# Carrying the last cross-attention sample steps into the gated-linear-attention stage

## The chip, the cores and the metric

The kernel runs on one core of a Trainium2 chip. The time is device microseconds of one launch; runs of one kernel are compared by their median. Before the change three runs gave 1443.68 us in the median (1443.25 to 1445.27).

A core has a matrix engine (PE, with its weight loads shown apart as PEld), a vector engine (DVE), a scalar/activation engine (ACT), a general engine (POOL) and a queue that issues transfers (SP). Each works through its own list of instructions in order and waits on semaphores for the others. Matrix results land in PSUM; here PSUM is cut into six buffers called `px` and two called `pz`.

## The reference, cut to what matters

One layer of a hybrid decoder is computed for 1024 prompt tokens and for 8 sample tokens that share the weights but have caches of their own:

```python
h = rmsnorm(x, norm_gain)
proj = h @ w_in                       # one combined projection, split into 10 parts
br_gla  = gla(q, k, v, log_a, S0) * silu(gla_g)          # 4 heads, dk 128, dv 256
br_pool = multiscale_pool(u, hist) * silu(pool_g)
br_x    = cross_attn(xq, mem_k, mem_v) * silu(xg)        # 4 heads, 256 memory tokens
merged  = sum_n sigmoid(merge_n) * (branch_n @ w_branch_n)
y       = rmsnorm(x + merged @ w_out, final_gain)
```

For the prompt, keys and values of the cross branch come from `mem_prompt`; for each of the 8 samples they come from its own cache (`cache_mem_k`, `cache_mem_v`), so the cross branch of the samples is 32 small attentions (8 samples by 4 heads) with 256 keys each. The GLA of the samples is one step of the recurrence on `state_gla`. Everything is float32.

## The kernel before, in words

**The main stream.** The projection is done in 40 pairs of 128-column blocks. Each pair takes seven block products (a Strassen-like scheme, operands named `a11`, `a12`, `s2`, `s1`, `s3`, `s4`, `a22`), and each product is done in two halves of 12 matmuls into `px` tiles (L242 to L244: every product is three matmuls of high and low parts). DVE and ACT split the next operands ahead (L223, L224, L305), and SP loads the weights (`raw`, L296, three buffers).

**The side streams.** After each half, `fill()` is called, and it lets side streams issue some of their steps between the halves. The side streams are Python generators that yield a cost for each step. `streams[0]` runs `cross_steps()` and then `gla_steps()`: it is given 493 units of work (`WORK_A`) over the halves 28 to 357, so that about 1.5 units are issued after each half. The order of steps on PE and SP is thus written out by hand (these two engines keep the order of the program). On DVE, ACT and POOL a scheduler orders the instructions at compile time; on the chip they too run in that fixed order.

**The cross stage** runs over 16 pieces (4 heads by 4 blocks of 256 tokens) in rounds `s`, shifted against each other as a pipeline:

- `cross_scores(s)`: 12 matmuls into `pz`, softmax on DVE and ACT.
- `cross_weights(s-1)` (L724): four PE transposes of the softmax result into `pz`, split by ACT into `pTh` and by DVE into `pTl`.
- `cross_values(s-2)`: 12 matmuls from `pTh`, `pTl` and the values (`mvsh`, `mkv`) into `pz`, evicted by ACT as `xo` (L736).

Rounds 16 and 17 are the run-out of this pipeline: round 16 has `values(14)` and `weights(15)`, round 17 only `values(15)`.

**The samples' cross chain**, `cross_sample(h)`, is a second generator, of 87 steps for the four heads. Each round has five places (`yield next(samples, 0)`) where one of its steps is issued. For one head: loads of keys `kc` and of the query `qb` broadcast from `xqs`, products with them on DVE (L777), a transpose of the scores (L791) with a softmax on DVE and ACT (`nm`, `ps`, L793 to L798), a transpose of that (L803) into `pm`, loads of the values `vc`, twice 16 small matmuls (L817) with an eviction to `cs`, and a transpose (L827) copied into `brs`. Steps that hold nothing but a cost (`yield 0.5`) are there to leave time between an operation and what reads it.

**The GLA stage**, `gla_steps()`, has 17 rounds: `gla_load` (`alc`, `kq` by SP), `gla_gates` (one matmul pair L907, then a chain of DVE and ACT operations), `gla_within` (L944 to L946, `ak` split), `gla_recur`, `gla_out`. Its own sample chain, `gla_sample(h)`, of 65 steps, is issued at up to four places in a round; it begins with `gla_rows(0)` (L1001).

All of these use the two `pz` buffers in turn, a ring of 14 SBUF tiles (`R`), and four SBUF tiles (`V`) for the samples' loads.

Of the kernel before, what the change touches and what calls it, by code (L numbers as in the profile page):

```python
# [24 lines left out]
NH = 4  # L25
# [22 lines left out]
def trunk_kernel(ctx: ExitStack, tc: tile.TileContext,  # L48
# [628 lines left out]
    def perm8(ap):  # L677
        return ap.rearrange("p (i j) -> p i j", i=2)

    cross = {}  # L680

    def cross_load(h):
        cross["raw", h] = [loaded(mkv_scr[o][h], [2, DV], "mkv") for o in range(2)]
# [1 line left out]
    def cross_memory(h):  # L685
        mk, mv = cross["raw", h]
        t = PZ()
        for i in range(2):
            for a in range(2):
                nc.tensor.transpose(t[:, i * NM + a * P:i * NM + (a + 1) * P], mk[:, a, i * P:(i + 1) * P], ident)  # L690
        cross["mk", h] = split_r(t.rearrange("p (i m) -> p i m", i=2), [2, NM], "mkT")
        cross["mv", h] = split_in(mv, [2, DV], "mvs")
# [7 lines left out]
    def cross_scores(h, c):  # L700
        xh, xl = cross["q", h, c]
        mh, ml = cross["mk", h]
        t = PZ()
        for j in range(2):
            for i in range(2):
                cs = slice(j * P, (j + 1) * P)
                mm3(t[:, j * NM:(j + 1) * NM], xh[:, i, cs], xl[:, i, cs], mh[:, i], ml[:, i], i == 0, i == 1)
        nm = tiny(2, "nm")
        nc.vector.tensor_reduce(nm, t.rearrange("p (j m) -> p j m", j=2), axis=AX.X, op=ALU.max, negate=True)
        p = R([2, NM], name="p")  # L710
        sm = tiny(2, "sm")
        for j in range(2):
            act(p[:, j], t[:, j * NM:(j + 1) * NM], AF.Exp, bias=nm[:, j:j + 1], accum_out=sm[:, j:j + 1])
        nc.vector.reciprocal(sm, sm)
        for j in range(2):
            nc.vector.tensor_scalar(p[:, j], p[:, j], sm[:, j:j + 1], None, op0=ALU.mult)
        cross["p", h, c] = p

    def cross_weights(h, c):
        p = cross["p", h, c]  # L720
        t = PZ()
        for a in range(2):
            for j in range(2):
                nc.tensor.transpose(t[:, (2 * a + j) * P:(2 * a + j + 1) * P], p[:, j, a * P:(a + 1) * P], ident)  # L724
        cross["pT", h, c] = split_r(t.rearrange("p (a t) -> p a t", a=2), [2, CT], "pT")
# [106 lines left out]
    def cross_steps():  # L832
        def scores(n):
            cross_scores(n // 4, n % 4)

        def memory(n):
            if n % 4 == 0:
                cross_memory(n // 4)

        def weights(n):  # L840
            cross_weights(n // 4, n % 4)

        def values(n):
            cross_values(n // 4, n % 4)

        samples = chain_of(cross_sample(h) for h in range(NH))
        cross_load(0)
        cross_memory(0)
        cross_fetch(0, 0)
        yield 2  # L850
        cross_queries(0, 0)
        cross_fetch(0, 1)
        for s in range(16 + 2):
            if s < 16:
                scores(s)
                yield 3
                if s + 1 < 16:
                    cross_queries(*divmod(s + 1, 4))
                if s + 2 < 16:
                    cross_fetch(*divmod(s + 2, 4))  # L860
            if s % 4 == 2 and s < 14:
                cross_load(s // 4 + 1)
            if s >= 1:
                yield next(samples, 0)
            if 0 <= s - 2:
                values(s - 2)
                yield 1.7
            if s >= 1:
                yield next(samples, 0)
            if s % 4 == 3 and s < 15:  # L870
                memory(s + 1)
                yield 2
            if 0 <= s - 1 < 16:
                weights(s - 1)
                yield 1.7
            for _ in range(3):
                if s >= 1:
                    yield next(samples, 0)
        yield from samples

    def chain_of(gens):
        for g in gens:
            yield from g
# [122 lines left out]
    def gla_sample(h):  # L1006

        if h == 0:
            gla_rows(0)
            yield 1  # L1010
        t = PZ()
        nc.tensor.matmul(t[:, :NS], lhsT=w2[:, h * P:(h + 1) * P], rhs=als, start=True, stop=True)
        z, m = tiny(NS, "gz"), tiny(NS, "gm")
        gate_exps(t[:, :NS], NS, h, z, m)
        dec = wk.tile([P, NS], F32, tag="as", name="as", bufs=2)
        act(dec, m, AF.Exp, scale=1.0 / TAU)
        nc.vector.tensor_scalar(qm[:, :, 0], smp_of(S_Q + h)[:, 0], DK ** -0.5, None, op0=ALU.mult)
        yield 2
        ks = smp_of(S_K + h)[:, 0]

        def fetch(b0):
            s0 = loaded(st_gla[b0:b0 + 2, h].rearrange("b k v -> k b v"), [2, DV], "s0", V)
            vb = V([2, DV], name="vb")
            nc.sync.dma_start(out=vb, in_=v_scr[h][b0:b0 + 2].partition_broadcast(P))
            return s0, vb

        def states(b0, s0, vb):
            for i in range(2):
                b = b0 + i
                nc.scalar.activation(s0[:, i], s0[:, i], AF.Copy, scale=dec[:, b:b + 1])  # L1030
                nc.vector.scalar_tensor_tensor(s0[:, i], vb[:, i], ks[:, b:b + 1], s0[:, i], op0=ALU.mult, op1=ALU.add)
            nc.gpsimd.dma_start(out=o_gla_s[b0:b0 + 2, h].rearrange("b k v -> k b v"), in_=s0)
            return s0

        os_ = R([2, DV], name="os")
        sq = wk.tile([P, 2], F32, tag="sqs", name="sqs", bufs=2)
        for i in range(2):
            fetched = [fetch(4 * i + b0) for b0 in (0, 2)]
            yield 1
            yield 0.5  # L1040
            s0 = []
            for b0 in (0, 2):
                s0.append(states(4 * i + b0, *fetched[b0 // 2]))
                yield 1.5
            yield 0.5
            t = PZ()
            for j in range(4):
                nc.tensor.matmul(t[32 * j:32 * j + 32, :DV], lhsT=qm[:, 4 * i + j, :], rhs=s0[j // 2][:, j % 2, :],
                                 start=True, stop=True)
            nc.scalar.activation(os_[:, i], t[:, :DV], AF.Copy)  # L1050
            nc.scalar.activation(t[:, :DV], t[:, :DV], AF.Square, accum_out=sq[:, i:i + 1])
            yield 1
        if h + 1 < NH:
            gla_rows(h + 1)
        r = rstd_of(sq, 1.0 / DV)
        for i in range(2):
            nc.scalar.activation(os_[:, i], os_[:, i], AF.Copy, scale=r[:, i:i + 1])
        yield 1
        yield 0.5
        t = PZ()  # L1060
        for i in range(2):
            for d in range(2):
                nc.tensor.transpose(t[:, (2 * i + d) * P:(2 * i + d + 1) * P], os_[:, i, d * P:(d + 1) * P], ident)
        for d in range(2):
            nc.vector.tensor_scalar(perm8(brs[0][:, 2 * h + d]), column0(t, d), ggain[:, 2 * h + d:2 * h + d + 1], None,
                                    op0=ALU.mult)
        yield 1.2

    def gla_steps():
        samples = chain_of(gla_sample(h) for h in range(NH))  # L1070
        N = 16
        gla_load(0, 0)
        gla_load(0, 1)
        gla_gates(0, 0)
        gla_values(0, 0)
        yield 5
        for n in range(N + 1):
            h, c = divmod(n, 4)
            ph, pc = divmod(n - 1, 4)
            if n + 1 < N:  # L1080
                gla_gates(*divmod(n + 1, 4))
                yield 5
            if n < N:
                gla_split(h, c)
                gla_within(h, 2 * c)
                yield 2
            if n > 0:
                gla_recur(ph, 2 * pc + 1)
                yield 2
                yield next(samples, 0)  # L1090
            if n < N:
                gla_within(h, 2 * c + 1)
                yield 2
                yield next(samples, 0)
                if n + 2 < N:
                    gla_load(*divmod(n + 2, 4))
                if n + 1 < N:
                    gla_values(*divmod(n + 1, 4))
                gla_recur(h, 2 * c)
                yield 2  # L1100
            if n > 0:
                gla_out(ph, pc)
                yield 2
            for _ in range(2):
                if n >= 1:
                    yield next(samples, 0)
        yield from samples


# [368 lines left out]
    for hf, order in enumerate(ORDERS):  # L1478
        for tb in order:
# [23 lines left out]
            n, a = hf, 0  # L1503
            for b in ends:
# [14 lines left out]
                n, a = n + 1, b  # L1519
# [46 lines left out]
```

## Time and profile before

| | |
|---|---|
| median of three runs | 1443.68 us (1443.25 to 1445.27) |
| the profiled execution: its own time | 1445.01 us |
| the profiled execution: span from first to last instruction | 1443.3 us |
| granted PE clock over the span, mean | 0.997 |
| PE busy | 1417.4 us (98%) |
| DVE, ACT, POOL busy | 916.2, 679.0, 222.1 us |

PE is the bound nearly everywhere; the 26 us in which it is idle are at the beginning, at the end, and in the cross stage. A row of the timeline gives start, duration, engine, source line, operation, output and inputs, and in brackets the idle time before it and whom it waited for. The list of waits gives, for a line, the total time waited, how often and the longest. A row of windows gives the busy time of each engine in a stretch, the granted PE clock and the share of the DMA engines that were busy. Durations of matmuls overlap (they are pipelined), so the pace is read from starts, not from durations.

### The profile page before, as it was taken

The page shows a single profiled execution, that of the slowest core. Times are in us where ns is not written, and L with a number is a line of the kernel's source. Part 1 is how long each engine was busy: PE and PEld are TensorE (multiplying, and loading weights), DVE is VectorE, ACT ScalarE, POOL GpSimd, SP SyncE. Part 2 cuts the span into 40 slices and gives each one's busy share as a digit, 9 for nine tenths or more (in the row PEclk, how much of TensorE's full clock was granted, in tenths as well). Part 3 has the DMA queues.
Part 4 walks back from the last instruction along what each step waited for, and adds up shares of the span by engine and source line. Part 5 has one row for each costly group of instructions (what it writes and reads, how often), then busy time and mean ns, then how long its engine had stood idle before and what let it go on. Part 6 is the DMA issues. An engine that isn't in the chain of part 4 may idle for free.

```text
span 1443.3 us, 28179 instructions
## 1 busy us (share of the span) xinstructions
PE 1417.4 (98%) x10689; PEld 1356.1 (94%) x10689; DVE 916.2 (63%) x2123; ACT 679.0 (47%) x1575; POOL 222.1 (15%) x401
## 2 busy tenths in 40 slices
PE   8999999999999999999999999999999999999998
PEld 6899999989899999999999999999999999999876
DVE  6954756666687777767766778785672434554436
ACT  6743544443465666656654445444472432233212
POOL 3211111124342121212221111111010000000000
PEclk9999999999999999999999999999999999999999
DMA  9355665656656363554654455454694777632633
GB/s 329 125 165 169 217 218 187 207 175 165 198 155 193 115 192 129 182 176 126 187 167 150 149 188 170 159 184 163 204 298 134 234 257 249 234 104 79 224 118 116
DMA packets 183507, 259.42 MB, mean 180 GB/s; under 512 B 22204, under 2 KB 132564, under 8 KB 183364
## 3 DMA queue, kind: packets, MB, share of 16 engines
q1 hardware_dynamic: 159900, 183.87, 41.5%
q0 software_dynamic: 23328, 73.56, 14.7%
q8 instruction: 84, 1.38, 0.4%
q14 instruction: 51, 0.42, 0.1%
q10 hardware_dynamic: 144, 0.20, 0.0%
HBM read 180.47 MB, written 77.56 MB: 179 GB/s over the span
## 4 chain that ended last, share of the span: by engine, by line
PE 88%; DMA 5%; DVE 5%; issue 1%; ACT 1%; SPq 0%; POOL 0%; DVEq 0%; ACTq 0%; POOLq 0%
PE px L242 25%; PE px L243 25%; PE px L244 25%; DMA qb<-xqs 3%; PE pz L244 2%; PE pz L243 2%; PE pz L242 2%; DMA raw<-in_w_in_dram 1%; DVE kc L777 1%; PE pz L963 1%; PE pz L404 1%; PE pz L944 1%; PE pz L817 1%; PE pz L946 1%; PE pz L907 0%
## 5 line engine op out<-in xcount | busy, mean ns | idle before, releaser
L244 PE MATMUL px<-bh,wbl 128*128 128x384 f32 (+1 forms) x576 | 184.1, 320 | 0.0
L243 PE MATMUL px<-bl,wbh 128*128 128x384 f32 (+1 forms) x576 | 184.1, 320 | 0.0
L242 PE MATMUL px<-bh,wbh 128*128 128x384 f32 (+1 forms) x576 | 183.7, 319 | 0.0
L554 ACT ACTIVATE r<-px 128x258 f32<-128x258 f32 x240 | 89.9, 375 | 47.4 <-PE px L244 46.9
L242 PEld LDWEIGHTS px<-bh,wbh 128*128 128x128 f32 x576 | 108.3, 188 | 0.0
L243 PEld LDWEIGHTS px<-bl,wbh 128*128 128x128 f32 x576 | 108.2, 188 | 0.0
L244 PEld LDWEIGHTS px<-bh,wbl 128*128 128x128 f32 x576 | 108.2, 188 | 0.0
L242 PE MATMUL px<-ot,s1h 128*128 128x258 f32 x320 | 94.1, 294 | 0.0
L242 PE MATMUL px<-o,a12h 128*128 128x258 f32 x320 | 93.4, 292 | 0.0
L242 PE MATMUL px<-ot,s3h 128*128 128x258 f32 x320 | 93.2, 291 | 0.0
L242 PE MATMUL px<-o,s4h 128*128 128x258 f32 x320 | 93.0, 291 | 0.2 <-DVE c L636 0.2
L242 PE MATMUL px<-o,a11h 128*128 128x258 f32 x320 | 92.8, 290 | 0.0
L242 PE MATMUL px<-ot,a22h 128*128 128x258 f32 x320 | 92.6, 289 | 0.0
L242 PE MATMUL px<-ot,s2h 128*128 128x258 f32 x320 | 92.2, 288 | 0.0
L243 PE MATMUL px<-o,a11h 128*128 128x258 f32 x320 | 91.1, 285 | 0.3 <-DVE o L224 0.3
L243 PE MATMUL px<-o,a12h 128*128 128x258 f32 x320 | 91.1, 285 | 0.0
L244 PE MATMUL px<-o,a12l 128*128 128x258 f32 x320 | 91.0, 284 | 0.0
L244 PE MATMUL px<-ot,s1l 128*128 128x258 f32 x320 | 90.9, 284 | 0.0
L243 PE MATMUL px<-ot,s1h 128*128 128x258 f32 x320 | 90.8, 284 | 0.0
L244 PE MATMUL px<-o,a11l 128*128 128x258 f32 x320 | 90.6, 283 | 0.0
L243 PE MATMUL px<-ot,s2h 128*128 128x258 f32 x320 | 90.1, 281 | 0.5 <-DVE ot L224 0.5
L243 PE MATMUL px<-ot,a22h 128*128 128x258 f32 x320 | 90.5, 283 | 0.0
(471 smaller groups left out, 4634.3 us busy)
## 6 DMA issues: line engine op xcount, KB each, us to landing
raw<-in_w_in_dram SPq DMA_DIRECT2D x80, 512.0 KB, 4.0
msc<-c POOLq DMA_DIRECT2D x24, 516.0 KB, 4.8
brsc<-c POOLq DMA_DIRECT2D x24, 516.0 KB, 3.7
sig<-msc SPq DMA_DIRECT2D x24, 516.0 KB, 6.0
brr<-brsc SPq DMA_DIRECT2D x48, 256.0 KB, 5.2
wbr<-in_w_branch_dram SPq DMA_DIRECT2D x24, 512.0 KB, 5.5
acc<-sig POOLq DMA_DIRECT2D x16, 516.0 KB, 5.2
acc<-acc SPq DMA_DIRECT2D x16, 516.0 KB, 7.0
```

Of the source, the lines that this page charges most:

```text
L242: nc.tensor.matmul(out, lhsT=lh, rhs=rh, start=start, stop=False, skip_group_check=more)
L243: nc.tensor.matmul(out, lhsT=lh, rhs=rl, start=False, stop=False, skip_group_check=more)
L244: nc.tensor.matmul(out, lhsT=ll, rhs=rh, start=False, stop=stop, skip_group_check=more)
L404: nc.tensor.matmul(t[:, :DV], lhsT=memT[k // 2][:, k % 2, a * P:(a + 1) * P], rhs=raw[k // 2][:, k % 2], start=k == 0, stop=k == NK - 1)
L554: nc.scalar.activation(r, acc[c][:, :QT], AF.Copy)
L777: nc.vector.tensor_tensor_reduce(kc[:, a, :], kc[:, a, :], qb[:, bb, :], scale=1.0, scalar=0.0, op0=ALU.mult, op1=ALU.add, accum_out=sc[:, ...
L817: nc.tensor.matmul(t[32 * j:32 * j + 32, :DV], lhsT=pm[:, a, 4 * i + j, :], rhs=vc[j][:, a, :], start=a == 0, stop=a == 1)
L944: nc.tensor.matmul(t[0:64, 0:P], lhsT=ki[:, 0:64], rhs=qi, start=True, stop=True)
L946: nc.tensor.transpose(t[:, P:2 * P], kt, ident)
L963: nc.tensor.matmul(to, lhsT=kiqi[:, 1, cs], rhs=st, start=False, stop=True)
```

## The change

In the rounds 16 and 17 of the cross stage the three places at the end of the round are no longer taken, and what is left of the samples' chain after the last round is not run out there but handed over in the list `later`. The GLA stage issues it ahead of its own sample steps. There the places at the end of a round become three in the rounds 0 to 4 (in round 0 there were none), and stay two in the later ones.

```diff
-    cross = {}
+    cross, later = {}, []
...
-            for _ in range(3):
+            for _ in range(3 if s < 16 else 0):
                 if s >= 1:
                     yield next(samples, 0)
-        yield from samples
+        later.append(samples)
...
     def gla_steps():
-        samples = chain_of(gla_sample(h) for h in range(NH))
+        samples = chain_of(later + [gla_sample(h) for h in range(NH)])
...
-            for _ in range(2):
-                if n >= 1:
-                    yield next(samples, 0)
+            for _ in range(3 if n < 5 else 2):
+                yield next(samples, 0)
         yield from samples
```

## The prediction

> **What bounds the kernel now.** I read the page's totals first, then the list of PE's waits, then the timelines of PE, DVE, ACT and SP around the end of the cross stage, and last the windows for the clock.
>
> ```profile
> span 1443.3 us, 28179 instructions
> PE 1417.4 (98%) x10689; PEld 1356.1 (94%) x10689; DVE 916.2 (63%) x2123; ACT 679.0 (47%) x1575; POOL 222.1 (15%) x401
> PE   8999999999999999999999999999999999999998
> ```
>
> PE is idle for 1443.3 - 1417.4 = 25.9 us of the span. The change removes no operation and adds none, so it can only gain where PE waits or runs at a lower clock, and only between the end of the cross stage and the end of the GLA stage. PE's list of waits for that stretch:
>
> ```profile
> PE pz L803 <- DVE ps L798: 2.4, 1, 2.4
> PE pz L243 <- DVE pTl L224: 1.5, 1, 1.5
> PE pz L724 <- ACT xo L736: 1.1, 1, 1.1
> PE pz L1001 <- DVE ak L224: 0.7, 1, 0.7
> 400.00:420.00 20.00, 20.00 (x164) 19.22 (x163) 16.71 (x46) 13.39 (x38) 10.19 (x17) 1.00 0.58 142
> 450.00:500.00 50.00, 50.00 (x412) 47.60 (x412) 39.01 (x107) 31.49 (x87) 10.38 (x19) 1.00 0.42 131
> ```
>
> Four waits, 5.7 us together. After them PE is busy without a gap (20.00 of 20.00, 50.00 of 50.00), so the rest of the GLA stage has nothing to give. The four in PE's order of time, with the steps between them:
>
> ```profile
> 356.16 0.39 PE L243 MATMUL pz<-pTl,mvsh 128*128 128x256 f32 x1 [1.48 <-DVE pTl L224]
> 357.56 0.28 PE L242 MATMUL px<-o,a12h 128*128 128x258 f32 x1
> 358.99 0.38 PE L791 MATMUL pz<-ident,sc 128*8 128x128 f32 x2
> 360.47 0.66 PE L724 MATMUL pz<-ident,p 128*128 128x128 f32 x4 [1.11 <-ACT xo L736]
> 363.71 0.28 PE L244 MATMUL px<-ot,s2l 128*128 128x258 f32 x1
> 366.39 0.26 PE L803 MATMUL pz<-ident,ps 8*128 8x8 f32 x2 [2.39 <-DVE ps L798]
> 369.25 1.54 PE L817 MATMUL pz<-vc,pm 128*32 128x256 f32 x16
> 372.27 0.28 PE L242 MATMUL pz<-pTh,mvsh 128*128 128x256 f32 x1
> 376.67 1.07 PE L817 MATMUL pz<-vc,pm 128*32 128x256 f32 x16
> 379.22 0.60 PE L827 MATMUL pz<-ident,cs 128*128 128x128 f32 x4
> 381.10 0.59 PE L907 MATMUL pz<-alc,w 128*128 128x256 f32 x2
> 396.90 0.38 PE L1001 MATMUL pz<-ident,smp 128*8 128x128 f32 x2 [0.66 <-DVE ak L224]
> ```
>
> A half of 12 matmuls takes 358.99 - 357.56 = 1.43 us. What made the wait of 2.39 us so long is seen on DVE, ACT and SP:
>
> ```profile
> 355.06 0.42 DVE L777 CUSTOM_DVE_ANT_0 kc<-kc,qb 128x256 f32<-128x256 f32 x1 [4.10 <-DMA qb<-xqs]
> 358.58 0.69 DVE L305 TENSOR_TENSOR ws<-raw 128x512 f32<-128x512 f32 x1
> 359.30 0.37 SPq L296 DMA_DIRECT2D raw<-in_w_in_dram  x1
> 363.75 0.69 DVE L305 TENSOR_TENSOR ws<-raw 128x512 f32<-128x512 f32 x1 [2.75 <-issue]
> 364.69 0.40 DVE L793 TENSOR_REDUCE nm<-pz 8x1 f32<-8x256 f32 x1
> 365.59 0.57 ACT L223 ACTIVATE pTh<-pz 128x512 fp32r<-128x512 f32 x1
> 365.90 0.34 DVE L798 TENSOR_SCALAR ps<-ps,sm 8x256 f32<-8x256 f32 x1
> 366.19 0.69 DVE L224 TENSOR_TENSOR pTl<-pz,pTh 128x512 fp32r<-128x512 f32 x1
> 373.07 0.69 DVE L224 TENSOR_TENSOR a22l<-raw,a22h 128x512 fp32r<-128x512 f32 x1 [4.67 <-ACT a22h L223]
> ```
>
> DVE waits 4.10 us for the last query broadcast; that pushes back its L305 at 358.58, which frees the buffer into which SP issues the next weights at 359.30; these are not there until DVE has stood 2.75 us at 363.75. Behind that, in DVE's fixed order, stand the sample softmax (`nm`, `ps`) and the split `pTl` of the last prompt piece. So L803 is late because of a late weight load, not because it follows L791 too closely.
>
> **The change part by part.** *Where steps go.* Of the chain's 87 steps the five places of rounds 1 to 17 take 85 and the tail 2. With 6 places fewer, 8 steps pass over, costing 0.5+1.2+0.5+0.5+1.2+0.5+0.5+1.2 = 6.1 units: both L817, the second `vc` load, L827 and the empty steps. At 493 units over 357 - 28 = 329 halves (1.5 a half) the GLA stage starts 6.1 / 1.5, about 4 halves, earlier. Stepping through the yields, after the half that ends with L791 and L724 come: two halves, `values(15)`; one half, L803 with the first `vc` loads; one half, the GLA loads and L907. Before it was: two halves, L803; one half, L817; one half, `values(15)`. In GLA the carried steps come at halves 159 (L817), 166 (L817) and 172 (L827), `gla_rows(0)` moves from 161 to 173, and from round 5 on the chain of `gla_sample` runs one step behind the old one. Total work is the same, so the pool stage starts at the same half, 357.
>
> *The waits before (1.48 and 1.11 us): 0.* The steps up to L724 are issued in the old order, so both stay, and with them DVE's 4.10 and 2.75 us.
>
> *L803's wait: taken over by `values(15)`, +0.3 us.* `values(15)` stands where L803 stood, two halves behind L724. Its first matmul needs `pTh`, ready at 365.59 + 0.57 = 366.16; its second needs `pTl`, ready at 366.19 + 0.69 = 366.88, against `ps` at 366.24. At `values(14)` such a first matmul went ahead alone and the second waited (356.16). So the second starts at about 366.93 where L803 started at 366.39: 0.54 us later, less one matmul already done at the slow pace (about 0.2): +0.3. L803 then finds `ps` ready. Bounds: if DVE and ACT keep their order, +0.6 at most; if the split came ahead of the softmax in their order, the wait could vanish: -2.4. I take +0.3, since everything that these two engines are given ahead of that point is unchanged.
>
> *The clock behind that wait: 0.*
>
> ```profile
> 366.00:369.00 3.00, 2.61 (x14) 2.62 (x14) 2.36 (x5) 1.21 (x4) 0.00 (x0) 0.64 0.65 221
> 369.00:372.00 3.00, 3.00 (x28) 1.90 (x28) 0.00 (x0) 0.38 (x1) 0.00 (x0) 0.79 0.05 13
> 122.57 0.38 PE L242 MATMUL pz<-mkTh,xqsh 128*128 128x256 f32 x1 [1.39 <-ACT xqsh L226]
> 123.36 0.39 PE L244 MATMUL pz<-mkTh,xq 128*128 128x256 f32 x1 [0.29 <-DVE xq L227]
> 120.00:130.00 10.00, 7.78 (x48) 7.15 (x47) 5.81 (x13) 4.49 (x11) 0.95 (x2) 0.83 0.71 211
> ```
>
> The granted clock falls to 0.64 and 0.79 there: 3 x 0.36 + 3 x 0.21 = 1.7 us lost. It also fell after 1.39 + 0.29 us at 122.57 (0.83 over 10 us: the same 1.7 us), but not after the single 1.48 at 356.16. A wait of some 2.5 us at the same place is clearly on the falling side, so the 1.7 us stay. [...] I go by the row.
>
> *L1001's wait: -0.66 us.* `gla_rows(0)` asked for a `pz` buffer one half after the second `within`, before DVE had split the `ak` in it. Now an empty step takes that place and the next asker is `recur(0)`, two halves behind, which is 1.43 us later than L1001's ask and so past the 0.66. Bounds -0.66 and 0.
>
> *L817 and L827 in GLA: 0.* Their PE work is only moved (16, 16 and 4 matmuls). Their `vc` have 12 and 7 halves to land, at 3.8 us from issue to landing, and PE sees ACT's and DVE's small copies (`cs`, `brs`) only through the `pz` buffers. The one tight spot is half 172 to 173: L827, `gla_rows(0)` and `gates(3)` ask for three `pz` tiles within one half, so `gates(3)` waits if DVE's copy into `brs` is over 1.5 us late. Bounds 0 and the 0.66 that L1001 paid for such a turn; I take 0, since now DVE has one half to do it.
>
> *The GLA loads on SP's queue: 0.*
>
> ```profile
> 359.76 13.30 SPq L670 DMA_DIRECT2D vc<-in_cache_mem_v_dram  x8
> 374.21 0.50 SPq L898 DMA_DIRECT2D alc<-als  x1
> alc<-als SPq DMA_DIRECT2D x3, 128.0 KB, 4.6
> vc<-in_cache_mem_v_dram SPq DMA_DIRECT2D x8, 256.0 KB, 3.8
> ```
>
> Eight `vc` loads blocked SP until 373.06, the second four waiting for L817. Now only four stand ahead of `alc` and `kq`, so these go out at about 362 and land by 367. L907 comes after 366.93, eleven matmuls, two halves and L803, about 373: 6 us of cover. The next weight load no longer stands behind the second `vc` but behind seven GLA loads, over 10 us earlier. The second `vc` now blocks SP until L817 at half 159; the weights emitted behind it (before half 163) are for the pair that begins about 20 halves on. On DVE the first gates fall into the idle 4.67 us that end at 373.07. POOL's write of `v_scr` has 9 halves (13 us) until it is read, instead of 11.
>
> *Sum:* 0 + 0.3 + 0 - 0.66 + 0 + 0 = -0.3 us. The profiled execution took 1445.01 us (1.7 over its span of 1443.3), 1.3 above the median; on the median of 1443.68 this makes 1443.4 us.
>
> **The rivals.**
>
> *Faster: the gap closes.* If `values(15)` found its operands ready, because DVE and ACT get another order or the weights come sooner, the 2.39 us, the 1.7 us of clock and the 0.66 go: 1443.7 - 4.8 = 1438.9 us. For it: two halves and L803's old wait lie between L724 and the point of need. Against: DVE's 2.75 us at 363.75 stand ahead of both results. Chance 0.13.
>
> *The wait stays, the clock holds.* The gap is now cut in two (2.2 us, a matmul, then 0.4), which may leave the clock up: 1443.4 - 1.7 = 1441.7 us. Against it is 122.57, where a gap cut in two brought the clock down. [...] Chance 0.05.
>
> *Slower: `pz` at half 173.* The two `pz` buffers turn faster while carried steps, `gla_rows(0)` and gates mix with `recur` and `within`. If `gates(3)`, or a `recur` behind it, waits as long as L803 did, 2.39 us, the clock falls too: 1443.4 + 2.4 + 1.7 = 1447.5 us. It decides from a gap of about 1.7 us on, the 1.39 + 0.29 that brought the clock down. For it: DVE is at 16.71 of 20 us there. Against: between 400 and 500 us PE waited for nothing. Chance 0.12.
>
> *It does not matter:* `values(15)` costs a little more, and `recur(0)` takes over L1001's wait: 1443.7 to 1444.3 us. Chance 0.08.
>
> **How the numbers follow.** The forecast has the remaining 0.62; its own range goes from 1443.7 - 0.66 - 0.4 (how far the fastest run lies below the median) = 1442.6 to 1443.7 + 0.6 + 0.66 (the upper bounds at `values(15)` and at `gates(3)`, nothing gained at L1001) = 1445.0. About 0.2% (2.9 us) is what a measurement of this kernel can tell from no change. Faster by more is the first rival alone (0.13), slower by more the third (0.12), within it the rest (0.75). The range reaches down to the first rival (1438.8) and up to a slower case with its full gap short of the full clock loss (1446.4), which leaves out about 0.1.
>
> **What would show it right or wrong.** Right: PE's waits near 366 name `pTh` or `pTl` before L242 or L243 of `values(15)`, about 2.2 + 0.4 us; none at L803 or L1001; the window from 366 to 372 still has a clock below 0.85; L907 comes some 8 us earlier, near 373, without a wait. Wrong: no wait there and a clock of 1.00 (first rival), or a new wait at L907, L944, L963 or L1001 past 373, above all for `brs` or `ak` (third). If DVE's order ahead of 366 differs from the old one, the step that everything hangs on has failed.

## The result: 0.4% slower, and the profile after

The changed kernel took 1450.06 us in the median (1445.54 to 1454.55) against 1444.12 us for the kernel before, run beside it on the same chip (1442.29 to 1446.82): a ratio of 1.0037 (95% interval 1.0023 to 1.0050), or 5.9 us more. The forecast of 1443.4 us and its range, 1446.4 us at the widest, are missed on the slow side. The profiled execution took 1450.53 us, 5.5 us more than that of before. The first lines of its page:

```profile
span 1448.8 us, 28181 instructions
PE 1417.9 (98%) x10689; PEld 1356.5 (94%) x10689; DVE 916.1 (63%) x2123; ACT 680.2 (47%) x1575; POOL 221.0 (15%) x401
```

The work is the same, as it had to be: PE has 10689 matmuls and 0.5 us more busy time. The rest must be idle time or clock. PE's list of waits between 340 and 520 us (total, how often, longest):

```profile
PE pz L242 <- ACT pTh L223: 2.4, 1, 2.4
PE pz L243 <- DVE pTl L224: 2.0, 2, 1.7
PE pz L1063 <- DVE ak L224: 1.9, 1, 1.9
PE pz L907 <- DMA alc<-als: 1.2, 1, 1.2
PE pz L724 <- ACT xo L736: 1.1, 1, 1.1
PE pz L944 <- ACT pz L977: 0.4, 1, 0.4
```

Against the four waits of before: L803 and L1001 are gone, `values(15)` (L242, L243) has L803's, and three are new, at L907, L1063 and L944, with a small one of 0.2 us at L1012. (Of L243's 2.0 us, 1.70 are `values(14)`, which waited 1.48 before.) The timeline of PE shows the first part of it in order:

```profile
364.45 0.38 PE L242 MATMUL pz<-pTh,mvsh 128*128 128x256 f32 x1 [2.44 <-ACT pTh L223]
365.18 0.58 PE L243 MATMUL pz<-pTl,mvsh 128*128 128x256 f32 x1 [0.34 <-DVE pTl L224]
...
369.42 0.29 PE L803 MATMUL pz<-ident,ps 8*128 8x8 f32 x2
...
371.19 0.59 PE L907 MATMUL pz<-alc,w 128*128 128x256 f32 x2
...
393.82 0.67 PE L907 MATMUL pz<-alc,w 128*128 128x256 f32 x2 [1.15 <-DMA alc<-als]
```

and the windows the clock behind the first wait (us; busy PE, PEld, DVE, ACT, POOL; granted clock; share of the DMA engines; GB/s):

```profile
360.00:366.00 6.00, 3.21 (x22) 2.81 (x22) 3.83 (x9) 2.09 (x6) 2.16 (x4) 0.90 1.03 340
366.00:372.00 6.00, 6.00 (x41) 5.79 (x41) 0.83 (x3) 1.27 (x3) 0.68 (x1) 0.82 0.63 218
```

This is what was forecast: 2.44 + 0.34 us in place of 2.39, L803 without a wait, the clock down to 0.82, the first L907 ten microseconds earlier than before (371.19 against 381.10) and no wait at it. The third L907, at 393.82, is the first surprise. SP's queue, after and then before:

```profile
372.71 16.05 SPq L296 DMA_DIRECT2D raw<-in_w_in_dram  x2
388.85 0.66 SPq L898 DMA_DIRECT2D alc<-als  x1
```

```profile
387.60 0.45 SPq L898 DMA_DIRECT2D alc<-als  x1
...
400.70 0.59 PE L907 MATMUL pz<-alc,w 128*128 128x256 f32 x2
```

The gates of this piece came 6.9 us earlier (393.82 against 400.70), their load did not (388.85 against 387.60). It stands on SP behind two weight loads, and the second of these waits 15.6 us until DVE, with an L305 that ends at 388.36, has released its buffer. Of 13.1 us between issue and use, 5.0 are left, and 1.15 of them are a wait.

The larger piece is at 504 us. The rows of PE, then of DVE and ACT ahead of it:

```profile
487.57 0.64 PE L1048 MATMUL pz<-s,pm 128*32 128x256 f32 x8
...
491.36 0.60 PE L907 MATMUL pz<-alc,w 128*128 128x256 f32 x2
...
504.24 0.66 PE L1063 MATMUL pz<-ident,os 128*128 128x128 f32 x4 [1.88 <-DVE ak L224]
...
505.34 0.47 PE L944 MATMUL pz<-kiqi 128*64 128x128 f32 x1 [0.44 <-ACT pz L977]
```

```profile
493.82 0.69 DVE L305 TENSOR_TENSOR ws<-raw 128x512 f32<-128x512 f32 x1 [1.30 <-DMA raw<-in_w_in_dram]
...
494.43 0.15 DVE L265 SCALAR_TENSOR_TENSOR rr<-rq,rr 128x2 f32<-128x2 f32 x1
...
494.62 0.91 ACT L1057 ACTIVATE os<-os,rr 128x256 f32<-128x256 f32 x2 [2.47 <-DVE rr L265]
...
495.96 0.45 ACT L890 ACTIVATE bz<-pz,vec 128x256 f32<-128x256 f32 x1
...
496.69 0.48 DVE L891 TENSOR_SCALAR bz<-pz,vec 128x256 f32<-128x256 f32 x1
...
503.67 0.42 DVE L224 TENSOR_TENSOR ak<-pz,ak 128x256 fp32r<-128x256 f32 x1
```

The same pieces before:

```profile
491.58 0.60 PE L1063 MATMUL pz<-ident,os 128*128 128x128 f32 x4
...
492.01 0.60 PE L907 MATMUL pz<-alc,w 128*128 128x256 f32 x2
...
493.88 0.48 DVE L891 TENSOR_SCALAR bz<-pz,vec 128x256 f32<-128x256 f32 x1
...
500.74 0.42 DVE L224 TENSOR_TENSOR ak<-pz,ak 128x256 fp32r<-128x256 f32 x1
```

Read from the bottom up: L1063 asks for a `pz` buffer that DVE has not split into `ak`. `ak` is late because the gates are: from L907 to DVE's L891 it takes 5.3 us (491.36 to 496.69), before 1.9 (492.01 to 493.88). The gates are late because ACT stood 2.47 us at L1057, the scaling of `os`, ahead of L890. L1057 waited for `rr`, which stands on DVE behind an L305 that waited for weights. Before, the transposes behind that scaling (L1063) were already done at 491.58, ahead of the gates. So, as these rows read, a 0.15 us operation behind a late weight load holds up the gates of a whole round. Then the clock:

```profile
505.00:508.00 3.00, 2.66 (x14) 2.33 (x15) 2.40 (x11) 2.87 (x10) 0.00 (x0) 0.50 1.00 331
508.00:511.00 3.00, 3.00 (x16) 3.00 (x16) 0.55 (x2) 0.42 (x2) 0.94 (x2) 0.50 1.02 319
```

Half speed for 6 us: 3.0 us lost, and 0.4 us more at the edges (a clock of 0.85 from 504 to 505 and of 0.73 from 511 to 512). With the waits of 1.88 and 0.44 this is some 5.7 us. A last new wait is at the end of the samples' chain, where before L1063 found its data ready:

```profile
753.86 0.84 PE L1063 MATMUL pz<-ident,os 128*128 128x128 f32 x4 [1.04 <-ACT os L1057]
```

That these places are all of it can be tested by lining up the two traces: the same block products start in both. Just ahead of the border, at 344.56 against 346.77 us (`s4`), the trace of after is 2.2 us ahead. This is no gain of the change: it comes from the clock drop at 122 us, which this execution did not have (1.7 us, see the end), and from waits that differ between the two traces (0.97 us at 169, 0.96 at 293 and 0.98 at 308 before; 1.86 in all from 161 to 169, 0.39 at 292 and none near 308 after). Behind the last moved step, at 776.11 against 770.23 (`s1`), it is 5.9 us behind. So 8.1 us are lost in between, and the rows make 8.0 of them: 1.3 around the stage border (+0.2 at `values(14)`, +0.4 at `values(15)`, +1.15 at `alc`, -0.66 at L1001, +0.2 at L1012, nothing in the clock), 5.7 at 504 us, and 1.0 at the end of the chain. These are two single executions; the medians differ by 5.9 us.

### The profile page after: what moved, and what is told of

Read it like the earlier page. It is cut to its first block, busy times and chain, and to the rows that moved or that the text cites. A ratio compares the mean times of both kernels' runs of the same rounds, so it can differ in the third digit from the quotient of the medians.

```text
span 1448.8 us, 28181 instructions
## 1 busy us (share of the span) xinstructions
PE 1417.9 (98%) x10689; PEld 1356.5 (94%) x10689; DVE 916.1 (63%) x2123; ACT 680.2 (47%) x1575; POOL 221.0 (15%) x401
## 4 chain that ended last, share of the span: by engine, by line
PE 84%; DVE 6%; DMA 6%; ACT 2%; issue 2%; SPq 0%; DVEq 0%; POOL 0%; ACTq 0%
PE px L242 24%; PE px L243 24%; PE px L244 24%; DMA qb<-xqs 2%; PE pz L243 2%; PE pz L244 2%; PE pz L242 2%; DMA raw<-in_w_in_dram 2%; DVE kc L777 1%; PE pz L963 1%; PE pz L944 1%; DMA x<-in_x_prompt_dram 1%; DVE ws L305 1%; DMA vb<-vs 1%; PE pz L946 0%
## 5 line engine op out<-in xcount | busy, mean ns | idle before, releaser
L243 PE MATMUL px<-bl,wbh 128*128 128x384 f32 (+1 forms) x576 | 184.1, 320 | 0.0
L242 PE MATMUL px<-bh,wbh 128*128 128x384 f32 (+1 forms) x576 | 183.7, 319 | 0.0
L242 PEld LDWEIGHTS px<-bh,wbh 128*128 128x128 f32 x576 | 108.3, 188 | 0.0
L243 PEld LDWEIGHTS px<-bl,wbh 128*128 128x128 f32 x576 | 108.2, 188 | 0.0
L242 PE MATMUL px<-o,a11h 128*128 128x258 f32 x320 | 94.9, 297 | 0.0
L242 PE MATMUL px<-ot,s1h 128*128 128x258 f32 x320 | 93.5, 292 | 0.0
L242 PE MATMUL px<-o,s4h 128*128 128x258 f32 x320 | 92.7, 290 | 0.2 <-DVE c L636 0.2
L242 PE MATMUL px<-ot,s3h 128*128 128x258 f32 x320 | 92.7, 290 | 0.0
L242 PE MATMUL px<-o,a12h 128*128 128x258 f32 x320 | 92.6, 289 | 0.0
L242 PE MATMUL px<-ot,s2h 128*128 128x258 f32 x320 | 92.4, 289 | 0.0
L243 PE MATMUL px<-o,a11h 128*128 128x258 f32 x320 | 92.1, 288 | 0.3 <-DVE o L224 0.3
L242 PE MATMUL px<-ot,a22h 128*128 128x258 f32 x320 | 92.1, 288 | 0.0
L243 PE MATMUL px<-ot,s2h 128*128 128x258 f32 x320 | 90.1, 282 | 0.5 <-DVE ot L224 0.5
L243 PE MATMUL px<-ot,a22h 128*128 128x258 f32 x320 | 90.5, 283 | 0.0
L243 PE MATMUL px<-ot,s1h 128*128 128x258 f32 x320 | 90.5, 283 | 0.0
L243 PE MATMUL px<-o,a12h 128*128 128x258 f32 x320 | 90.5, 283 | 0.0
L244 PE MATMUL px<-ot,s3l 128*128 128x258 f32 x320 | 90.4, 283 | 0.0
```

What stands on the lines that cost most here:

```text
L242: nc.tensor.matmul(out, lhsT=lh, rhs=rh, start=start, stop=False, skip_group_check=more)
L243: nc.tensor.matmul(out, lhsT=lh, rhs=rl, start=False, stop=False, skip_group_check=more)
L244: nc.tensor.matmul(out, lhsT=ll, rhs=rh, start=False, stop=stop, skip_group_check=more)
```

## Experiments

The theory that they began with (A): from round 5 on the samples' chain stands one step behind its old place, this puts the scaling of `os` just ahead of the gates and the L1063 behind it in front of a late `ak`; undo the lag and the loss goes. Its rival, the prediction's third: the two `pz` buffers simply turn faster with another asker among them, whatever ACT and DVE do there. A second question was the price of giving `values(15)` L803's wait, and a third whether the delay behind that wait can be removed in another way. All ratios are against the kernel before in runs beside it (its median was 1443.44, 1443.81, 1442.43 and 1443.53 us in the four groups e1 to e4, e5 to e8, e9 to e11, e12 to e14).

### e1: the lag undone by a place in round 0

```diff
-            for _ in range(3 if n < 5 else 2):
+            for _ in range(4 if n == 0 else 3 if n < 5 else 2):
```

> The changed kernel with four instead of three places at the end of GLA round 0, so that from the end of round 4 on every step of the GLA samples stands where it stood before the change. Theory A (the changed kernel loses its time because the samples' chain runs one step behind: the step that scales `os` now stands right ahead of the gates of round 6, ACT waits there for DVE, the gates and the split of `ak` come late, and PE waits at L1063 and L944 for 1.9 + 0.4 us, plus 3.4 us of clock): the waits near 504 us are gone, the clock there is 1.00, and the time is 5 to 6 us below the changed kernel, about 1444 to 1445 us. Theory B (it is the earlier start of the GLA stage, with the gates that wait for `alc`, and what follows from it): still 1448 to 1451 us.

1448.25 us, ratio 1.0038 (1.0024 to 1.0052). The waits at 504 are gone (PE is busy without a gap from 485 to 520 us, at a clock of 1.00), but another wait has come:

```profile
395.61 3.63 PE L817 MATMUL pz<-vc,pm 128*32 128x256 f32 x16 [4.66 <-DMA vc<-in_cache_mem_v_dram]
```

The fourth place of round 0 puts the second L817 right behind the first, before its `vc` can land. The time therefore says nothing about the lag; the trace says that the wait at 504 depends on which steps stand there.

### e2: half of the change, fewer places, nothing carried

```diff
-            for _ in range(3):
+            for _ in range(3 if s < 16 else 0):
```

> The kernel before with only the six places of the cross rounds 16 and 17 taken away; the samples' chain is run out ahead of the GLA stage, which is as before. Theory A: no loss from the GLA samples, since their steps stand as before; values(15) waits for pTh and pTl in place of L803 (about 2.4 + 0.3 us), and L1001 waits about 0.7 us as before: 1443.5 to 1446 us, the 8 steps run one after the other adding at most 1 us. Theory B: also no loss, as GLA starts at its old half. A time above 1447 us would mean that the cross part alone costs something that neither theory has.

1446.92 us, ratio 1.0023 (1.0009 to 1.0037), above the expected 1443.5 to 1446. The rest of the chain now runs out right behind `values(15)`, and its loads have no time to land:

```profile
PE pz L817 <- DMA vc<-in_cache_mem_v_dram: 2.2, 3, 1.3
```

So the carry does what it says for `vc`: in the changed kernel no L817 waits.

### e3: the lag alone

```diff
-        samples = chain_of(gla_sample(h) for h in range(NH))
+        samples = chain_of([[0]] + [gla_sample(h) for h in range(NH)])
```

> The kernel before with one empty step of no cost at the head of the GLA samples' chain, so that its steps come one place later throughout and nothing else changes. Theory A: a wait of 2 to 2.5 us appears at L1063 and L944 in GLA round 5 (near 500 us) with the clock at one half for some 6 us: 1448 to 1450 us. Theory B: no change, 1443 to 1445 us.

1444.05 us, ratio 1.0003 (0.9992 to 1.0014): theory A falls. The old kernel with one empty step ahead of its chain has no wait at 504 us. What differs is the neighbourhood: here L1048 (the matmuls of the samples' outputs, whose result is scaled) runs four halves ahead of the scaling, in the changed kernel one half. The third place in round 4, the last round that has three, packs L1048, the scaling and the gates of round 6 one behind the other. This is theory A' below: not the lag, the crowding. The lag does cost something, at the end of the chain:

```profile
747.37 0.84 PE L1063 MATMUL pz<-ident,os 128*128 128x128 f32 x4 [0.74 <-ACT os L1057]
```

### e4 and e5: the scaling left out, and the place moved away

The changed kernel without the scaling of `os` for head 0, whose output is then unscaled:

```diff
-        r = rstd_of(sq, 1.0 / DV)
-        for i in range(2):
-            nc.scalar.activation(os_[:, i], os_[:, i], AF.Copy, scale=r[:, i:i + 1])
+        if h > 0:
+            r = rstd_of(sq, 1.0 / DV)
+            for i in range(2):
+                nc.scalar.activation(os_[:, i], os_[:, i], AF.Copy, scale=r[:, i:i + 1])
```

> The changed kernel without the normalisation of `os` for head 0 of the samples (the small chain for its reciprocal root and the two scalings on ACT, about 1 us of ACT work, are left out for that head); all steps stay at their places and L1063 still asks for its `pz` between recur and within. Theory A: ACT no longer waits for DVE ahead of the gates of round 6, `ak` is split in time, the waits near 504 us are gone: 1444 to 1445.5 us. Rival C (the turn of the two `pz` buffers: the mere request of L1063 between recur and within makes PE wait, however the gates run): the wait at L1063 stays, 1449 to 1451 us.

1446.09 us, ratio 1.0017 (1.0008 to 1.0026). Its list of waits from 340 to 520 us has no L1063 any more:

```profile
PE pz L907 <- DMA alc<-als: 2.5, 1, 2.5
PE pz L242 <- ACT pTh L223: 2.2, 1, 2.2
...
PE pz L944 <- ACT pz L977: 1.0, 1, 1.0
```

L1063 still asks for `pz` at the same place between the same askers, so the rival (the turn of the buffers by itself) is out as the cause of that wait: it came through the scaling. (L944 still waits for a buffer, 0.97 us here.) The trace also parts the scaling from the late weights ahead of it. L305 stood 2.40 us for its weights here, longer than the 1.30 us of the changed kernel, and yet L890 began 0.7 us after L907 (491.84 to 492.58) instead of 4.6 us (491.36 to 495.96). So late weights alone do not hold up the gates; whether the scaling would with weights in time was not run. The same with all work in place, the changed kernel with its last third place moved from round 4 to round 2:

```diff
-            for _ in range(3 if n < 5 else 2):
+            for _ in range(4 if n == 2 else 3 if n < 4 else 2):
```

> The changed kernel with its five extra places at other rounds: four at the end of round 2 and two at the end of round 4, instead of three and three. From round 4 on every step of the GLA samples then stands where it stood in the kernel with only the lag of one step, so L1048 of head 0 comes four halves ahead of the step that scales `os` instead of one, while that step and L1063 keep their places (halves 213 and 220). Theory A' (not the lag, but L1048, the scaling and the gates of round 6 following one another closely, because of the third place in round 4): the waits at L1063 and L944 near 504 us and the clock drop go, 4 to 6 us below the changed kernel: 1444.5 to 1446.5 us, with the wait for `alc` and the one at values(15) left. Theory A (the lag): unchanged, 1449 to 1451 us.

1446.50 us, ratio 1.0020 (1.0004 to 1.0037). From 485 to 520 us PE is busy without a gap at a clock of 1.00. What is left at the border, beside `values(15)`:

```profile
PE pz L907 <- DMA alc<-als: 2.6, 1, 2.6
```

### e6 and e8: the loads of the gates brought forward

The changed kernel with the loads of GLA piece 2 issued right behind the gates of round 1, and then the same together with the moved place:

```diff
                 gla_gates(*divmod(n + 1, 4))
+                if n == 0:
+                    gla_load(0, 2)
...
-                if n + 2 < N:
+                if 0 < n < N - 2:
```

> The changed kernel with the three loads of GLA piece 2 issued right behind the gates of round 1, seven halves earlier, so that on SP they stand ahead of the weight load that waits for DVE. Theory B: the wait of L907 for `alc` (1.2 us in the changed kernel, 2.5 us in the kernel without the scaling of head 0) goes, and with it the clock drop that follows it in part of the runs: 1 to 3 us below the changed kernel, 1447 to 1449 us. If that wait does not matter: unchanged, about 1450 us.

> The changed kernel with both edits, the place moved from round 4 to round 2 and the loads of GLA piece 2 ahead of the weight load. If these two make up the loss: the time of the kernel before or a little less, 1442.5 to 1444.5 us, with the wait at values(15) as the only long one left after 350 us. If something else of the carry costs time: above 1446 us.

Alone: 1449.93 us, ratio 1.0043 (1.0028 to 1.0058), no gain. The wait for `alc` is gone, L1063's 1.89 us at 504 stays, and a new one comes right behind. Its cause was not followed further; in e8, whose steps up to there are the same, it is 0.33 us.

```profile
402.41 1.07 PE L817 MATMUL pz<-vc,pm 128*32 128x256 f32 x16 [1.55 <-ACT pz L977]
```

With the place moved: 1445.02 us, ratio 1.0015 (1.0002 to 1.0029), the best form of the carry. After 350 us PE's list has only the following, 1.1 at L724 and 0.69 at the last L1063:

```profile
PE pz L242 <- ACT pTh L223: 2.3, 1, 2.3
PE pz L243 <- DVE pTl L224: 1.4, 2, 1.1
...
PE pz L817 <- ACT pz L977: 0.3, 1, 0.3
PE pz L1012 <- DVE ak L224: 0.2, 1, 0.2
```

This kernel and e6 differ by the place alone and ran beside each other; the ratio of their means is 0.9973 (0.9953 to 0.9994, worked out from the spread of both), so the place in round 4 is worth 3.9 us (1 to 7), which has room for the 5.7 of the trace. What the `alc` wait is worth stays open: from the moved place alone to both it is 0.9993 (0.9973 to 1.0012).

### e7, e9, e10 and e11: time given to the late split instead

The kernel before with an empty step between `weights(15)` and what follows, to see whether the wait at L803 can be bought off without any carry. First 3 units more in all; then 1.5 and 3, taken back from the first cost of the GLA stage (`yield 5`), so that GLA starts at its old half:

```diff
                 yield 1.7
+                if s == 16:
+                    yield 3.0
```

> The kernel before with 3 units of empty cost (two halves of products, 2.9 us) put in between weights(15) and L803; what follows comes two halves later. If the reading of that wait is right (the softmax and pTl are late by a fixed time, because of a late weight load), L803 finds its operand there: its 2.4 us and the 1.7 us of clock behind it go, 4 us below the kernel before: 1439 to 1441 us. If the wait only moves with the step (the results come later too): 1443 to 1445 us.

> The kernel before with 1.5 units of empty cost (one half, 1.43 us) between weights(15) and L803, and 1.5 units less behind the first gates of the GLA stage, so that from the gates of round 1 on all steps stand where they stood. If the wait at L803 is a fixed lateness of DVE (and the loss with two halves of gap came from the shift of everything behind): its 2.4 us become about 1.0 us, under what brings the clock down, so 1.4 + 1.7 us are gained: 1440.5 to 1442 us. If the results move with the step: 1443.5 to 1444.5 us.

> The same with 3 units (two halves) at both places: the wait at L803 goes altogether, as it did with the gap of two halves before, and the steps from the gates of round 1 on stand as before, so the waits that came with that shift (the hist load, ak and others) are not there: 1439.5 to 1441 us. Against it stands that the first gates now have 5 instead of 7 halves until within(0); if they are late by then, PE waits 0.5 to 3 us there and the time is 1441 to 1444 us.

The first took 1454.28 us, ratio 1.0085 (1.0072 to 1.0098): no wait at L803 any more, but everything in GLA stands two halves later, and from 520 us on PE waits twice for `ak` (3.6 us) and for the pool stage's load:

```profile
PE pz L1129 <- DMA hist<-in_state_pool_dram: 4.6, 1, 4.6
```

With the units taken back: 1442.75 us, ratio 0.9997 (0.9983 to 1.0012), and 1442.13, ratio 1.0003 (0.9991 to 1.0015), no difference that shows: the first lies between its two expectations, the second in the range of its worse one. With 1.5 units the wait has been shared out (lines behind 875 have moved by two, so L1003 is the old L1001):

```profile
PE pz L1003 <- DVE ak L224: 1.4, 1, 1.4
...
PE pz L817 <- DMA vc<-in_cache_mem_v_dram: 1.0, 1, 1.0
...
PE pz L803 <- DVE ps L798: 0.6, 1, 0.6
```

With 3 units the trace has no wait at L803 and no clock below 1.00 from 354 to 400 us. Its waits there are 1.6 us at L1003 and 1.1 each at L243 and L724, 3.8 us in place of the 5.7 and the 1.7 us of clock in the kernel before. The times do not show these 3.6 us: the interval leaves room for a gain of 1.3. The profiled execution was the shortest of its twelve (1437.88 us), and one and the same wait brings the clock down in some traces only (see the end); whether this explains it stays open.

Then the best form of the carry with the 1.5 units ahead of `values(15)`, taken back in the same way:

> The changed kernel with the place moved to round 2, the loads of GLA piece 2 ahead, and the gap of 1.5 units, here between weights(15) and values(15), with 1.5 units less behind the first gates. If the wait at values(15) is the same fixed lateness as that at L803: from 2.3 + 0.3 us to about 1.2 us and mostly without the clock drop, 2.5 to 3 us below the kernel without the gap: 1442 to 1443 us. If not: 1444.5 to 1445.5 us.

1448.68 us, ratio 1.0041 (1.0030 to 1.0053). `values(15)` waits only 0.45 + 0.34 us, and the first gates, at the place where the prediction had 6 us of cover, wait for their load, which went out only at 365.32, behind a weight load at 364.91:

```profile
369.03 1.19 PE L909 MATMUL pz<-alc,w 128*128 128x256 f32 x2 [3.62 <-DMA alc<-als]
```

### e12 to e14: the root of the waits, the last query broadcast

If the late `qb` load (DVE's 4.10 us in the prediction's rows) is what makes the split late, a kernel without it has no wait to take over, and the carry is measured by itself. For the last pair of samples of head 3 the query tile of the pair ahead is used, one load of 256 KB less:

```diff
-        def fetch(b2):
+        def fetch(b2, old=None):
...
+            if old is not None:
+                return kc, old
...
-                kcs, qb = fetch(b2 + 1)
+                kcs, qb = fetch(b2 + 1, qb if h == 3 and b2 == 2 else None)
```

> The kernel before, but the last pair of samples of head 3 uses the query tile of the pair ahead of it, so that one load of 256 KB (`qb`) is left out. Theory D (all four waits of PE between 354 and 367 us come down from DVE's wait of 4.1 us for that load, which makes the split, the eviction, the next weight load and the softmax late): DVE's wait at L777 shrinks to 1 us or less, the waits at values(14), L724 and L803 (1.5, 1.1 and 2.4 us) mostly go with the clock drop behind them: 1437.5 to 1440 us. If each of them has a cause of its own: at least two stay, 1441.5 to 1443.5 us.

> The changed kernel with the same load left out. The wait at values(15) (2.4 + 0.3 us, with the clock) should go like that at L803. Theory A' (the loss lies in round 4's third place, at L1063 near 504 us) and B (`alc` behind the weight load): their waits stay, as they do not hang on that load, and the distance to the same edit on the kernel before stays at 4.5 to 6 us: 1443 to 1445.5 us. If the loss comes down from the late data at values(15): the distance shrinks to 2 us or less, 1439 to 1441.5 us.

> The changed kernel with the place moved to round 2, the loads of GLA piece 2 ahead, and the same load left out. Without these two causes and without the late data there is nothing known left that the carry costs: within 1 us of the same edit on the kernel before, 1437.5 to 1440.5 us. If it stays 1.5 us or more above, the carry has a cost that no wait seen so far explains.

On the kernel before: 1440.26 us, ratio 0.9976 (0.9964 to 0.9988), 3.3 us less, which counts only as a measure of the waits since a load, and its traffic, is missing. For the kernel before the root is shown: `values(14)` and L724 no longer wait, and L803 waits 0.5 us, for another operation (L805 is the old L803, L1003 the old L1001). What stays is

```profile
PE pz L1003 <- DVE ak L224: 0.7, 1, 0.7
PE pz L805 <- ACT r L554: 0.5, 1, 0.5
```

The traces differ by 6.2 us there (5.7 of waits and 1.7 of clock against 1.2), the medians by 3.3 (by the interval 1.7 to 5.2).

On the kernel after: 1445.46 us, ratio 1.0017 (1.0005 to 1.0030). The new waits of the GLA stage are still there:

```profile
PE pz L909 <- DMA alc<-als: 2.1, 1, 2.1
PE pz L1065 <- DVE ak L224: 1.9, 1, 1.9
```

`values(15)` waits only 0.79 + 0.45 us in this trace, and the clock stays at 1.00 from 360 to 372 us. So without the late query the carry costs 5.2 us (1445.46 - 1440.26; with it 5.9): the main loss is the carry's own and does not come from the wait that it was laid around.

The carry with moved place and early loads: 1441.60 us, ratio 0.9992 (0.9981 to 1.0002), 1.3 us above the same edit on the kernel before (with the query 1.2), a little more than the 1 us expected. But here the late data are not gone: DVE waits 2.28 us for a load of keys (`kc`) instead, `values(15)` waits 1.46 + 0.34 us, and the clock is 0.50 from 363 to 366. So this run does not settle what the best form would cost with data in time.

## Why the prediction was wrong

*The waits before* and *L803's wait: taken over by `values(15)`*: right. The first two waits stayed (1.70 and 1.09 against 1.48 and 1.11), the third was taken over at +0.4 us (forecast +0.3), and DVE kept its order up to the split.

*The clock behind that wait*: right for this execution. 6 x 0.10 + 6 x 0.18 = 1.7 us lost between 360 and 372, as before. But the second rival (the clock holds) is not out: in the trace of e4 the clock stayed at 1.00 behind 2.22 + 0.34 us at the same place.

*L1001's wait: -0.66*: right, it is gone. A wait of 0.2 us for `ak` is new at L1012.

*The GLA loads on SP's queue: 0*: wrong. The step checked the first two pieces, whose loads had only four `vc` ahead of them, and was right for them (no wait at 371.19). It had the next weight load go out over 10 us earlier, but that load went out at 372.71, 1.1 us earlier than before (373.79): it waits for DVE to release a buffer, and DVE had moved forward by no more than that (its `a22l` at 371.99 against 373.07). From the third piece on the GLA loads stand behind such weight loads, while L907 had moved 6.9 us forward: 1.15 us here, 2.1 to 2.6 in e4, e5 and e13. The price in the median stays open.

*"From round 5 on the chain of `gla_sample` runs one step behind the old one"*: this sentence carried no price, and was the place of the loss. The working followed the moved steps L817 and L827 through *`L817 and L827 in GLA: 0`*, and these cost nothing indeed. It did not ask what the steps of `gla_sample` meet at their new places: the term that was left at 0 is +5.7 us at 504 in the trace (3.9 by the runs of e8 against e6), from the scaling of `os` between L1048 and the gates, and +1.0 at the end of the chain. The lag of one step alone is not the fault, as e3 shows; it takes the third place in round 4 beside it, as e5 shows. That PE waited for nothing between 400 and 500 us was read as room to spare; it did not say how near DVE and ACT were to being late there.

The third rival had the kind of loss right (a wait for a `pz` buffer, then the clock, 1447.5 us), with a chance of 0.12, but put it at half 173, where L827, `gla_rows(0)` and `gates(3)` meet and nothing waited. The gap of about 1.7 us from which it let the clock fall is not a limit: the same gap at 122 us left the clock at 0.83 in the trace of before and at 1.00 in that of after.

The sum of the best form: +0.24 at `values(15)` (2.29 + 0.34 - 2.39), -0.66 at L1001, +0.33 at L817, +0.2 at L1012 and +0.7 at the last L1063 is +0.8 us, against 1.2 by the medians (by the ratio's interval 0.3 to 4.2). So even without the two mistakes the change gave nothing that could be measured: it passes a wait from one instruction to the next, and the delay is made on DVE and in the loads.

## What to carry to other kernels

When steps of a hand-ordered chain are moved, every later step of the chain moves too: look, for each of them, at what DVE and ACT have queued around its new place, above all for a small operation (here 0.15 us) that stands behind a load and ahead of something that many wait for. An engine that moves forward takes its need for loads forward, not the loads (here the third gates came 6.9 us earlier and the issue of their load 1.3 us later): compare issue and use of each load that follows, not only the first. A wait whose cause is on another engine goes on to the next asker (here L803's 2.39 us became the 2.44 + 0.34 us of `values(15)`), so look for the late load first (here 256 KB of queries, worth 3.3 us) before laying PE's steps around it.

## What the runs showed of the hardware

In the trace of after the granted clock dropped behind short gaps: it was 0.50 from 365 to 368 us behind 2.44 + 0.34 us at 364, and 0.50 from 505 to 511 behind 1.88 + 0.44 us. But it does not drop each time. The wait at 122 us is the same in the traces of before, after, e5, e10, e12, e13 and e14 (1.39 us, then 0.28 or 0.29). Behind it the clock over 120 to 130 us was 0.83 in four of them, before (48 matmuls in the prediction's row), e5, e12 and e14, and 1.00 in the other three. The rows of after:

```profile
122.53 0.39 PE L242 MATMUL pz<-mkTh,xqsh 128*128 128x256 f32 x1 [1.39 <-ACT xqsh L226]
```

```profile
120.00:130.00 10.00, 7.32 (x57) 6.70 (x56) 6.64 (x14) 4.45 (x11) 0.95 (x2) 1.00 0.70 211
```

The same holds for the longer gap at `values(15)`. Behind 2.29 + 0.34 us the clock of e8 was 0.50 from 366 to 369; behind 2.22 + 0.34 us that of e4 was still 1.00:

```profile
363.00:366.00 3.00, 2.66 (x20) 2.46 (x21) 1.97 (x3) 1.51 (x4) 0.00 (x0) 1.00 1.06 367
```

The same gap cost 1.7 us of clock in one trace and nothing in another; what decides between the two was not shown.

So the clock's part in the price of one wait cannot be read from one trace. Runs of one kernel differ by some 4 us either way, and the longer ones tend to have the lower mean clock (e9, median 1442.75: 1437.48 us at 0.999, 1446.50 at 0.996). The prediction's terms of 0.3 and 0.66 us could be seen in a trace, but not in a time.
